# The recurrent gates of the first two tiles moved behind the products of the low-rank queries

## The chip, the cores and the metric

The program runs on one core of a Trainium2 chip, as one launch. The metric is the device time in microseconds (us), the median of several runs. The core has five engines, each with its own stream of instructions: PE (TensorE, matrix products), DVE (VectorE), ACT (ScalarE, with loadable function tables), POOL (GpSimd) and SP (SyncE, which here issues nearly all DMAs). They wait for each other by semaphores.

## The reference, cut to what matters

Two blocks follow each other on 1024 tokens of width 1024, in fp32: a block of two layers (a mixer of a gated recurrence and low-rank attention, then a state-space layer), and a second block (two feed-forward parts and a mixer). The change lies in the first mixer only:

```
proj = x @ w_in
x_rnn, gate, c_q, c_kv, k_rope = split(proj)          # 512, 1024, 256, 128, 32 columns
x_rnn = causal_conv(x_rnn, conv_w, conv_b)            # 4 taps
r = sigmoid(x_rnn @ w_a + b_a);  i = sigmoid(x_rnn @ w_x + b_x)
log_a = -8 * r * softplus(-lam);  a = exp(log_a)
u = sqrt(-expm1(2 * log_a)) * (i * x_rnn)
h[t] = a[t] * h[t-1] + u[t]                           # y_rnn
q  = rmsnorm(c_q, q_norm) @ w_uq
kv = rmsnorm(c_kv, kv_norm) @ w_ukv
... attention over 8 heads, then concat(y_rnn, y_mla) * silu(gate) @ w_out
```

## The kernel before, in words

Activations of the mixer stand feature by feature: a tile has 128 features (partitions) by 1024 tokens. A product that must be near fp32 is made from three: every factor is split into a high and a low part (`split`, lines 140 and 141: ACT copies the high part, DVE subtracts it), and high by high, high by low and low by high are added up in PSUM. A projection of one tile (`proj_fm`, line 185) is thus 8 blocks of features by 3 products by 2 halves of the tokens, 48 matmuls of 512 columns, into one PSUM tile `pa` of 1024 columns. The pool of these, `psA`, has two buffers; a second pool, `psB`, has four buffers `pb` of 512 columns.

`layer_a` starts with the projections of the first two recurrent tiles together (line 446, one product into each of the two `pa` buffers). `rnn(m)` then finishes recurrent tile m, for m from 0 to 3:

- the convolution `conv4`: ACT writes the first tap from `pa` (line 354), DVE adds three taps, each read from `pa` again (line 356);
- the gates: four plain fp32 matmuls of 512 columns from the convolved tile into `pb` (line 462), each followed by a Sigmoid on ACT (line 463);
- the rest: `i * xc` on DVE (line 464), Exp, Tanh and Sqrt on ACT (465 to 467), and on DVE lines 468 to 472, the last one the scan over the tokens. Sigmoid, Exp with Tanh, and Sqrt are in different function tables, so that ACT loads a table between them.

`low(...)` projects the low-rank queries (two tiles) or keys and values (one tile): product, Copy and Square on ACT (486, 487), a sum of squares by 8 matmuls with one column each (489), a root on DVE over 8 columns (493 to 283), that root spread over partitions by matmuls (501), a scaling on DVE (504) and a split. The program calls rnn(0), rnn(1), low for the queries, rnn(2), low for the keys, rnn(3), the rotary part and four gate tiles. Weights come by SP's DMAs into two staging buffers and are split into four buffers `whi` and four `wlo`.

The order on each engine is not the order of the calls: a scheduler places instructions by a model of their times, and may let a later product run ahead of something that waits. `turn(K, trace)` (line 168) takes this freedom away on PE: what `trace` issues is put behind the last PE instruction written before it.

Of the kernel before, what the change touches and what calls it, by code (L numbers as in the profile page):

```python
# [18 lines left out]
P = 128  # L19
# [3 lines left out]
NK = D // P  # L23
# [75 lines left out]
def anchor(K, engine=None):  # L99

    for i in reversed(K.nc.cur_bb.bb.instructions):
        if i.engine == (engine or K.pe):
            return i
    return None
# [33 lines left out]
def split(K, hi, lo, src, eng=None):  # L138

    K.nc.scalar.activation(hi, src, AF.Copy)  # L140
    (eng or K.nc.vector).tensor_tensor(lo, src, hi.bitcast(F32), ALU.subtract)  # L141


def scale_rows(K, st, gain, k0, n):

    for k in range(n):
        K.nc.scalar.activation(st[:, k, :], st[:, k, :], AF.Copy, scale=col(K, gain, k0 + k))  # L147


def wload(K, src, a, b, gain=None, k0=0):  # L150

    n = a * b
    st = K.pwst.tile([P, 1024], F32, tag="wst", name=K.nm("wst"))
    hi = K.pwh.tile([P, 1024], F32R, tag="whi", name=K.nm("whi"))
    lo = K.pwl.tile([P, 1024], F32R, tag="wlo", name=K.nm("wlo"))
    K.nc.sync.dma_start(st[:, :n].rearrange("p (a b) -> p a b", a=a), src)
    if gain is not None:
        scale_rows(K, st[:, :n].rearrange("p (a b) -> p a b", a=a), gain, k0, a)
    split(K, hi[:, :n], lo[:, :n], st[:, :n])
    v = lambda t: t[:, :n].rearrange("p (a b) -> p a b", a=a)  # L160
    return v(hi), v(lo)


def kp(ap):
    return ap.rearrange("(k p) c -> p k c", p=P)


def turn(K, trace):

    with K.tc.issue_after(anchor(K)):  # L170
        trace()


def proj_list(K, ps, terms, mid=None):


    n = len(terms)
    with ExitStack() as st:
        for k, (wh, wl, xh, xl) in enumerate(terms):
            if mid is not None and k == n // 2:  # L180
                turn(K, mid)
                st.enter_context(K.tc.issue_after(anchor(K)))
            for m, (w, x) in enumerate(((wh, xh), (wh, xl), (wl, xh))):
                for h in (0, 512):
                    K.nc.tensor.matmul(ps[:, h:h + 512], w, x[:, h:h + 512],  # L185
                                       start=k == 0 and m == 0, stop=k == n - 1 and m == 2)


def proj_fm(K, ps, w, xt, nk=NK, mid=None):
    proj_list(K, ps, [(w[0][:, k, :], w[1][:, k, :], xt("h", k), xt("l", k)) for k in range(nk)], mid)  # L190
# [34 lines left out]
def col(K, name, j=0, n=1, p0=0, p1=P):  # L225
    c0, _ = _PK[name]
    return K.pk[p0:p1, c0 + j:c0 + j + n]
# [36 lines left out]
def rsqrt_col(K, out, v, n, scale, eps, mul=1.0, tag="rs"):  # L264

    V = K.nc.vector
    t = K.small(3 * n, f"{tag}{n}", bufs=2 if n == 1 else 1)
    h, y, c = (t[:, j * n:(j + 1) * n] for j in range(3))  # L270
    k = 1.5 ** 0.2
    f = -0.5 / (mul * mul)
    V.tensor_scalar(h, v, scale * f, eps * f, ALU.mult, ALU.add)

    magic = 1597463007.0 - 2.0 ** 30 - 2.0 ** 22 + 2.0 ** 23 * math.log2(k) / 3
    V.tensor_scalar(y.bitcast(I32), h.bitcast(I32), -0.5, magic, ALU.mult, ALU.add)

    if n == 1:

        step = lambda o, i, a, b: V.tensor_scalar(o, i, a, b, ALU.add, ALU.mult)  # L280
        square = lambda: V.tensor_scalar(c, y, y, h, ALU.mult, ALU.mult)
    else:
        step = lambda o, i, a, b: V.scalar_tensor_tensor(o, i, a, b, ALU.add, ALU.mult)

        def square():
            V.tensor_tensor(c, y, y, ALU.mult)
            V.tensor_tensor(c, c, h, ALU.mult)

    square()
    step(y, c, 1.5 * k ** (2.0 / 3), y)  # L290
    square()
    step(h, c, k ** 2 * 5.0 / 3, c)
    step(out, h, k ** 4 * 1.25, y)
# [51 lines left out]
def conv4(K, out, src, wname, j, nm, bname, copy=False):  # L345


    nc = K.nc
    w = lambda k: col(K, wname, k * nm + j)
    raw = src  # L350
    if copy:
        raw = K.pwl.tile([P, 1024], F32, tag="wlo", name=K.nm("raw"))
        nc.scalar.activation(raw, src, AF.Copy)
    nc.scalar.activation(out, src, AF.Identity, bias=col(K, bname, j), scale=w(3))
    for s in (1, 2, 3):
        nc.vector.scalar_tensor_tensor(out[:, s:], raw[:, :T - s], w(3 - s), out[:, s:], ALU.mult, ALU.add)
# [58 lines left out]
def layer_a(K, I, XT, get):  # L415
    nc = K.nc

    w_in = kp(I["w_in"])
# [31 lines left out]
    def rnn(m):  # L450
        if m < 2:
            a = first[m]
        else:
            a = K.A()
            proj_fm(K, a, wload(K, w_in[:, :, m * P:(m + 1) * P], NK, P), get)
        pa, pb = K.P2(), K.P2()
        xc, t, i, s = pa[:, 0, :], pa[:, 1, :], pb[:, 0, :], pb[:, 1, :]
        conv4(K, xc, a, "a_conv_w", m, 4, "a_conv_b")
        for dst, w, b in ((t, m, "ga_b"), (i, 4 + m, "gx_b")):
            for h in (slice(0, 512), slice(512, 1024)):  # L460
                g = K.B()
                nc.tensor.matmul(g, wgv[:, w, :], xc[:, h], start=True, stop=True)
                nc.scalar.activation(dst[:, h], g, AF.Sigmoid, bias=col(K, b, m))
        nc.vector.tensor_tensor(i, i, xc, ALU.mult)
        nc.scalar.activation(xc, t, AF.Exp, scale=lam[:, 8 + m:9 + m])
        nc.scalar.activation(t, t, AF.Tanh, scale=lam[:, 4 + m:5 + m])
        nc.scalar.activation(s, t, AF.Sqrt)
        nc.vector.scalar_tensor_tensor(s, xc, 1.0, s, ALU.add, ALU.mult)
        nc.vector.tensor_tensor(i, i, s, ALU.mult)
        nc.vector.scalar_tensor_tensor(xc, xc, 1.0, t, ALU.add, ALU.mult)  # L470
        nc.vector.tensor_scalar(xc, xc, -1.0, 1.0, ALU.mult, ALU.add)
        nc.vector.tensor_tensor_scan(s, xc, i, 0.0, ALU.mult, ALU.add)
        return s


    rst = {}

    def low(c0, nt, name, scale):
        raws = []
        rq = K.Q2()  # L480
        ssq = K.B()
        for m in range(nt):
            a = K.A()
            proj_fm(K, a, wload(K, w_in[:, :, c0 + m * P:c0 + (m + 1) * P], NK, P), get)
            raw, sq = rq[:, m, :], K.S()
            nc.scalar.activation(raw, a, AF.Copy)
            nc.scalar.activation(sq, a, AF.Square)
            for i in range(NT):
                nc.tensor.matmul(ssq[:, m * 8 + i:m * 8 + i + 1], sq[:, i * P:(i + 1) * P], K.ones, start=True, stop=True)
            raws.append(raw)  # L490
        r = K.small(8, "rst" + name, bufs=1)
        v = K.small(8, "rsv" + name, bufs=1)
        nc.vector.tensor_copy(v, ssq[:, 0:8])
        for m in range(1, nt):
            nc.vector.tensor_tensor(v, v, ssq[:, m * 8:m * 8 + 8], ALU.add)
        rsqrt_col(K, r, v, 8, scale, 1e-6)
        outs = [K.Q2(F32R) for _ in range(nt)]
        for h in range(2):
            b = K.B()
            for q in range(4):  # L500
                nc.tensor.matmul(b[:, q * P:(q + 1) * P], r[:, 4 * h + q:4 * h + q + 1].to_broadcast([P, P]), K.ident, start=True, stop=True)
            for m in range(nt):
                rw = raws[m][:, h * 512:h * 512 + 512]
                nc.vector.scalar_tensor_tensor(rw, rw, col(K, name, m), b, ALU.mult, ALU.mult)
                split(K, outs[m][:, 0, h * 512:h * 512 + 512], outs[m][:, 1, h * 512:h * 512 + 512], rw)
        return outs

    hs = [rnn(0)]
    hs.append(rnn(1))
    cq = low(1536, 2, "qn", 1.0 / 256)  # L510
    hs.append(rnn(2))
    ckv = low(1792, 1, "kvn", 1.0 / 128)
    hs.append(rnn(3))
    cs, n1, n2 = K.R2(), K.L(), K.L()
    sin_tables(K, I["pos"], cs[:, 0, :], cs[:, 1, :], n1, n2)
    kr = K.A()
# [1446 lines left out]
def tile_two_blocks(ctx, tc, I, out):  # L1963
# [4 lines left out]

    XT, get = new_xt(K)
    ydram, zd = layer_a(K, I, XT, get)  # L1970
    XT = _Late(K)
    layer_a_out(K, I, ydram, zd, x1, XT)
# [46 lines left out]
```

## Time and profile before

| what | us |
|---|---|
| median of 3 runs (3287.15 to 3292.08) | 3291.51 |
| the profiled execution: time | 3285.83 |
| its span | 3284.10 |
| PE busy in it (94% of the span) | 3077.9 |
| DVE busy (67%) | 2211.5 |
| ACT busy (49%) | 1625.5 |
| POOL busy (24%) | 778.3 |

The times of rows are counted from the start of the span. PE is the engine that is nearly always busy, so in a stage where nothing else ends last a change counts by what it adds to or takes from PE's idle time and PE's clock. The first mixer's part up to the heads of attention takes the first 258 us.

### The profile page before, as it was taken

Reading aid. Unit: us, or ns where it says so; the run is one execution under the profiler, and the core shown is the slowest. Engines: PE = TensorE matmul, PEld = TensorE weight load, DVE = VectorE, ACT = ScalarE, POOL = GpSimd, SP = SyncE. Lnnn points to the kernel's source line nnn. Section 1 sums busy time; section 2 is a strip of 40 time slices with the busy share of each in tenths; the row PEclk is TensorE's granted clock in tenths of the full one; section 3 lists DMA queues with packets and bytes.
Section 4 is the critical chain, followed back from the end, with each engine's and each line's share of the span. In section 5 each row is a group of like instructions: output and inputs, shape, how many; then the busy total and the mean of one; then the engine's idle time right before and its main releaser. Section 6 shows DMA issues by size and latency. Waiting matters only on the chain. (4 is left out here: it accounts for less than half of the span.)

```text
span 3284.1 us, 42186 instructions
## 1 busy us (share of the span) xinstructions
PE 3077.9 (94%) x15560; PEld 2568.7 (78%) x15560; DVE 2211.5 (67%) x3637; ACT 1625.5 (49%) x2945; POOL 778.3 (24%) x487
## 2 busy tenths in 40 slices
PE   8999889999999989789999899899999799999998
PEld 6887777888897878578778777788787688888776
DVE  6537777356757556887775789736666955555997
ACT  5526543445555522655555443642565755554442
POOL 0000001113222221522233534100000432332543
PEclk9998999999999999899999999999999899999999
DMA  4157442334344565323332620354564322224223
GB/s 130 55 182 231 123 132 86 88 83 124 83 117 92 170 176 162 99 97 116 109 123 77 225 84 33 128 179 174 152 169 140 131 84 90 77 84 152 105 84 116
DMA packets 349567, 398.98 MB, mean 121 GB/s; under 512 B 21168, under 2 KB 279344, under 8 KB 349360
## 3 DMA queue, kind: packets, MB, share of 16 engines
q1 hardware_dynamic: 324016, 379.50, 37.1%
q10 hardware_dynamic: 25344, 16.78, 1.6%
q8 instruction: 123, 2.02, 0.3%
q14 instruction: 84, 0.69, 0.1%
HBM read 279.29 MB, written 116.92 MB: 121 GB/s over the span
## 5 line engine op out<-in xcount | busy, mean ns | idle before, releaser
L141 DVE TENSOR_TENSOR wlo<-wst,whi 128x1024 fp32r<-128x1024 f32 (+1 forms) x190 | 232.1, 1224 | 355.6 <-ACT whi L140 337.5
L185 PE MATMUL pa<-x,whi 128*128 128x512 f32 x1568 | 429.2, 395 | 1.8 <-DVE l L141 0.8
L140 ACT ACTIVATE whi<-wst 128x1024 fp32r<-128x1024 f32 (+1 forms) x190 | 180.1, 948 | 345.5 <-PE pa L185 86.0
L147 ACT ACTIVATE wst<-wst,pk 128x128 f32<-128x128 f32 (+1 forms) x816 | 251.7, 391 | 187.9 <-DMA wst<-in_ffn_w_in_dram 120.7
L185 PEld LDWEIGHTS pa<-x,whi 128*128 128x128 f32 x1568 | 292.0, 189 | 64.1 <-DVE x L141 1.8
L185 PE MATMUL pa<-x,wlo 128*128 128x512 f32 x784 | 244.2, 392 | 4.0 <-DVE wlo L141 4.0
L1325 PE MATMUL pa<-x,whi 128*128 128x512 f32 (+1 forms) x736 | 221.7, 384 | 4.2 <-ACT p L679 2.0
L1325 PE MATMUL pb<-x,whi 128*128 128x512 f32 (+1 forms) x736 | 224.0, 381 | 0.3 <-DVE r L141 0.3
L1404 PE MATMUL pa<-wlo,whi 128*128 128x512 f32 x768 | 188.5, 403 | 14.6 <-DVE wlo L141 12.7
L1404 PE MATMUL pb<-wlo,whi 128*128 128x512 f32 x744 | 182.2, 403 | 14.2 <-DVE wlo L141 14.2
L1288 POOL TENSOR_TENSOR s<-wst 128x512 f32<-128x512 f32 x44 | 57.9, 1317 | 561.2 <-ACT wst L147 525.4
L1404 PEld LDWEIGHTS pa<-wlo,whi 128*128 128x128 f32 x768 | 148.4, 194 | 52.3 <-DVE wlo L141 18.4
L1404 PEld LDWEIGHTS pb<-wlo,whi 128*128 128x128 f32 x744 | 143.9, 195 | 48.5 <-DVE wlo L141 18.2
L185 PEld LDWEIGHTS pa<-x,wlo 128*128 128x128 f32 x784 | 147.0, 188 | 38.8 <-DVE wlo L141 7.4
L937 POOL TENSOR_TENSOR s<-s,p 128x1024 f32<-128x1024 f32 x32 | 65.6, 2051 | 440.7 <-DMA s<-d 324.5
L1325 PEld LDWEIGHTS pa<-x,whi 128*128 128x128 f32 x736 | 136.8, 190 | 32.0 <-issue 2.6
L1325 PEld LDWEIGHTS pb<-x,whi 128*128 128x128 f32 x736 | 135.9, 188 | 26.9 <-DVE r L141 0.5
L140 ACT ACTIVATE whi<-s 128x1024 fp32r<-128x1024 f32 x88 | 93.0, 1057 | 117.5 <-POOL s L1289 67.1
L891 PE MATMUL pa<-whi,x 128*128 128x256 f32 x512 | 147.9, 289 | 0.0
L892 PE MATMUL pa<-wlo,x 128*128 128x256 f32 x512 | 145.1, 283 | 1.9 <-DVE wlo L141 1.9
L893 PE MATMUL pa<-whi,x 128*128 128x256 f32 x512 | 144.8, 283 | 0.0
L681 POOL TENSOR_TENSOR p<-p,q 128x1024 f32<-128x1024 f32 x8 | 21.1, 2641 | 515.0 <-DVE p L680 476.4
(591 smaller groups left out, 8056.9 us busy)
## 6 DMA issues: line engine op xcount, KB each, us to landing
wst<-in_ffn_w_in_dram SPq DMA_DIRECT2D x88, 512.0 KB, 3.8
d<-p SPq DMA_DIRECT2D x82, 512.0 KB, 3.5
d<-l SPq DMA_DIRECT2D x67, 512.0 KB, 3.9
x<-d SPq DMA_DIRECT2D x128, 256.0 KB, 5.4
p<-d SPq DMA_DIRECT2D x46, 512.0 KB, 4.7
wst<-in_s_w_in_dram SPq DMA_DIRECT2D x40, 512.0 KB, 4.0
s<-d SPq DMA_DIRECT2D x32, 512.0 KB, 9.6
l<-d SPq DMA_DIRECT2D x24, 512.0 KB, 5.6
```

The costliest lines, as they stand in the source:

```text
L140: K.nc.scalar.activation(hi, src, AF.Copy)
L141: (eng or K.nc.vector).tensor_tensor(lo, src, hi.bitcast(F32), ALU.subtract)
L147: K.nc.scalar.activation(st[:, k, :], st[:, k, :], AF.Copy, scale=col(K, gain, k0 + k))
L185: K.nc.tensor.matmul(ps[:, h:h + 512], w, x[:, h:h + 512], start=k == 0 and m == 0, stop=k == n - 1 and m == 2)
L681: nc.gpsimd.tensor_tensor(z, z, b, ALU.add)
L891: nc.tensor.matmul(o, xh, wh, start=k == 0, stop=False)
L892: nc.tensor.matmul(o, xh, wl, start=False, stop=False)
L893: nc.tensor.matmul(o, xl, wh, start=False, stop=k == NK - 1)
L937: nc.gpsimd.tensor_tensor(mv, mv, per_head(csT, P), ALU.subtract)
L1288: G(s1, a21, a22, ALU.add)
L1325: nc.tensor.matmul(p, l[:, k, :], r[:, k, :], start=k + m == 0, stop=k == 3 and m == 2)
L1404: nc.tensor.matmul(bank[j], th[:, a + o:a + o + P], tw[:, b:b + 512], start=c + m == 0, stop=c == n - 1 and m == 2)
```

## The change

`rnn` becomes a generator with a stop behind the convolution and a second one at its result. The first two tiles are convolved first. `low` for the queries gets a list of two traces, one for each of its two products: behind the sum of squares of a product comes the rest of one recurrent tile (gates, Exp, Tanh, Sqrt, scan). Each product of `low`, and each of these rests, is put in place with `turn`. rnn(2) and rnn(3) run through at once, as before; `low` for the keys has no list, but its product stands in a `turn` as well.

```diff
@@ -456,6 +456,7 @@
         conv4(K, xc, a, "a_conv_w", m, 4, "a_conv_b")
+        yield
         for dst, w, b in ((t, m, "ga_b"), (i, 4 + m, "gx_b")):
...
         nc.vector.tensor_tensor_scan(s, xc, i, 0.0, ALU.mult, ALU.add)
-        return s
+        yield s
...
-    def low(c0, nt, name, scale):
+    def low(c0, nt, name, scale, behind=()):
...
-            proj_fm(K, a, wload(K, w_in[:, :, c0 + m * P:c0 + (m + 1) * P], NK, P), get)
+            w = wload(K, w_in[:, :, c0 + m * P:c0 + (m + 1) * P], NK, P)
+            turn(K, lambda: proj_fm(K, a, w, get))
...
             raws.append(raw)
+            if behind:
+                turn(K, behind[m])
...
-    hs = [rnn(0)]
-    hs.append(rnn(1))
-    cq = low(1536, 2, "qn", 1.0 / 256)
-    hs.append(rnn(2))
+
+    hs = []
+    pair = [rnn(0), rnn(1)]
+    for r in pair:
+        next(r)
+    cq = low(1536, 2, "qn", 1.0 / 256, [lambda r=r: hs.append(next(r)) for r in pair])
+    hs.append(list(rnn(2))[-1])
     ckv = low(1792, 1, "kvn", 1.0 / 128)
-    hs.append(rnn(3))
+    hs.append(list(rnn(3))[-1])
```

On PE, behind the two products of the first tiles (`pa_199`, `pa_200`), there stood before the gates of tile 0 (from `p_297`), the first product of the queries (`pa_353`), and the gates of tile 1 (from `p_324`) in its last pair:

```order
L446 MATMUL pa_200<-x_115,wlo_128 128x512
L462 MATMUL pb_303<-p_297,r_197 128x512
...
L462 MATMUL pb_312<-p_297,r_197 128x512
L185 MATMUL pa_353<-x_114,whi_355 128x512 x2
...
L185 MATMUL pa_353<-x_115,wlo_356 128x512
L462 MATMUL pb_330<-p_324,r_197 128x512
```

There now stand the first product of the queries (`pa_311`), its sum of squares, the gates of tile 0, and the second product (`pa_398`):

```order
L446 MATMUL pa_200<-x_115,wlo_128 128x512
L185 MATMUL pa_311<-x_114,whi_313 128x512 x2
...
L185 MATMUL pa_311<-x_115,wlo_314 128x512 x2
L491 MATMUL pb_310<-ones,s_366 128x1 x8
L463 MATMUL pb_377<-p_297,r_197 128x512
...
L463 MATMUL pb_386<-p_297,r_197 128x512
L185 MATMUL pa_398<-x_114,whi_400 128x512 x2
```

The gates of tile 0 moved behind a product and its sum of squares, and this sum, which stood in the middle of the next product, now stands directly behind its own.

Further on, on PE, the product of recurrent tile 2 is `pa_523`, its convolved tile `p_578`, and the product of the keys `pa_607`. Before, that product stood on both sides of the queries' root (line 501) and of the gates of tile 2:

```order
L185 MATMUL pa_607<-x_114,whi_609 128x512 x2
...
L501 MATMUL pb_512<-ident,rstqn_485 128x128 x4
L185 MATMUL pa_607<-x_116,whi_609 128x512 x2
...
L462 MATMUL pb_584<-p_578,r_197 128x512
...
L185 MATMUL pa_607<-x_117,whi_609 128x512 x2
```

Now the end of `pa_523` (with the last gate of tile 1, `pb_473`), the root, the gates and the whole product follow one another:

```order
L463 MATMUL pb_473<-p_303,r_197 128x512
L185 MATMUL pa_523<-x_117,whi_525 128x512
L185 MATMUL pa_523<-x_115,wlo_526 128x512 x2
L505 MATMUL pb_501<-ident,rstqn_485 128x128 x4
L505 MATMUL pb_512<-ident,rstqn_485 128x128 x4
L463 MATMUL pb_584<-p_578,r_197 128x512
...
L463 MATMUL pb_593<-p_578,r_197 128x512
L185 MATMUL pa_607<-x_114,whi_609 128x512 x2
```

No matmul of the keys' product stands ahead of the gates of tile 2 any more.

On DVE, at the same place, the three taps of tile 2 (line 356, from `pa_523`) stood before among the scalings of the queries (line 504), and the second half of tile 1 had been done long before:

```order
L356 SCALAR_TENSOR_TENSOR p_578<-pa_523,pk,p_578 128x1023
L356 SCALAR_TENSOR_TENSOR p_578<-pa_523,pk,p_578 128x1022
L504 SCALAR_TENSOR_TENSOR q_351<-q_351,pk,pb_501 128x512 x2
L356 SCALAR_TENSOR_TENSOR p_578<-pa_523,pk,p_578 128x1021
L504 SCALAR_TENSOR_TENSOR q_351<-q_351,pk,pb_512 128x512 x2
```

Now the taps stand apart, and ahead of the last of them is line 469 for tile 1 (`p_303`, `p_304`), which reads the Sqrt:

```order
L508 SCALAR_TENSOR_TENSOR q_309<-q_309,pk,pb_512 128x512 x2
L356 SCALAR_TENSOR_TENSOR p_578<-pa_523,pk,p_578 128x1023
L141 TENSOR_TENSOR q_499<-q_309,q_499 128x512
...
L141 TENSOR_TENSOR q_500<-q_309,q_500 128x512
L356 SCALAR_TENSOR_TENSOR p_578<-pa_523,pk,p_578 128x1022
L469 SCALAR_TENSOR_TENSOR p_304<-p_303,p_304 128x1024
L356 SCALAR_TENSOR_TENSOR p_578<-pa_523,pk,p_578 128x1021
```

The last tap of tile 2 moved behind an instruction of tile 1 that waits for ACT. Lines from 459 on are numbered 1 to 7 higher in the changed kernel.

## Rows read from the trace of the kernel before

**Rows 1.** Waits of PE, longest in total: line, releaser, us in total, times, longest.

```profile
PE pb L462 <- issue: 6.3, 1, 6.3
```

**Rows 2.** Timeline of PE: start, us, instructions merged, in brackets the idle time before.

```profile
32.69 0.39 PE L446 MATMUL pa<-x,wlo 128*128 128x512 f32 x1
39.38 6.10 PE L462 MATMUL pb<-p,r 128*128 128x512 f32 x8 [6.31 <-issue]
...
50.80 1.07 PE L185 MATMUL pa<-x,whi 128*128 128x512 f32 x4
...
52.16 1.07 PE L185 MATMUL pa<-x,whi 128*128 128x512 f32 x4
...
71.96 0.62 PE L185 MATMUL pa<-x,wlo 128*128 128x512 f32 x2
...
88.31 1.95 PE L501 MATMUL pb<-ident,rstqn 128*128 128x128 f32 x16
90.02 0.71 PE L185 MATMUL pa<-x,whi 128*128 128x512 f32 x2
```

**Rows 3.** Timeline of DVE, the convolutions, the recurrence and the scalings.

```profile
36.69 2.59 DVE L356 SCALAR_TENSOR_TENSOR p<-pa,pk,p 128x1022 f32<-128x1022 f32 x2
...
53.68 1.23 DVE L468 SCALAR_TENSOR_TENSOR p<-p,p 128x1024 f32<-128x1024 f32 x1 [2.27 <-ACT p L467]
54.94 1.23 DVE L469 TENSOR_TENSOR p<-p 128x1024 f32<-128x1024 f32 x1
...
89.63 1.40 DVE L504 SCALAR_TENSOR_TENSOR q<-q,pk,pb 128x512 f32<-128x512 f32 x2
...
93.45 2.49 DVE L141 TENSOR_TENSOR q<-q,q 128x512 fp32r<-128x512 f32 x4
```

**Rows 4.** Timeline of ACT: gates, tables, and what follows a product.

```profile
44.66 0.69 ACT L463 ACTIVATE p<-pb,pk 128x512 f32<-128x512 f32 x1 [0.80 <-PE pb L462]
45.24 1.21 ACT L354 ACTIVATE p<-pa,pk 128x1024 f32<-128x1024 f32 x1
46.33 0.69 ACT L463 ACTIVATE p<-pb,pk 128x512 f32<-128x512 f32 x1
...
48.93 1.16 ACT L465 ACTIVATE p<-p,lam 128x1024 f32<-128x1024 f32 x1 [0.61 <-DVE p L464]
...
51.29 1.28 ACT L467 ACT_TABLE_LOAD   x1
52.59 1.06 ACT L467 ACTIVATE p<-p 128x1024 f32<-128x1024 f32 x1
...
72.16 1.06 ACT L140 ACTIVATE whi<-wst 128x1024 fp32r<-128x1024 f32 x1 [3.52 <-PE pa L185]
73.13 1.01 ACT L486 ACTIVATE q<-pa 128x1024 f32<-128x1024 f32 x1
74.03 1.02 ACT L487 ACTIVATE s<-pa 128x1024 f32<-128x1024 f32 x1
...
85.85 1.19 ACT L354 ACTIVATE p<-pa,pk 128x1024 f32<-128x1024 f32 x1
...
90.41 1.35 ACT L140 ACTIVATE q<-q 128x512 fp32r<-128x512 f32 x2 [3.36 <-DVE q L504]
```

**Rows 5.** Stretches: length, busy us of PE, PEld, DVE, ACT, POOL, granted clock, DMA.

```profile
39.30:45.00 5.70, 5.62 (x9) 2.49 (x9) 0.00 (x0) 2.77 (x4) 0.00 (x0) 0.56 0.17 48
...
1230.80:1238.00 7.20, 7.19 (x26) 5.80 (x27) 6.08 (x11) 1.74 (x4) 1.04 (x1) 0.76 0.40 130
...
1653.70:1661.00 7.30, 7.28 (x34) 6.04 (x35) 7.30 (x12) 5.77 (x14) 0.00 (x0) 1.00 0.34 99
```

**Rows 6.** Timeline of PE, two waits of 2.5 to 2.7 us elsewhere.

```profile
1230.81 0.49 PE L941 MATMUL pb<-q 128*128 128x128 f32 x2 [2.73 <-ACT r L1000]
...
1653.72 0.70 PE L1325 MATMUL pa<-r,whi 128*128 128x512 f32 x2 [2.48 <-DVE p L1334]
```

**Rows 7.** The stretch that holds the heads of attention, columns as in rows 5.

```profile
260.00:500.00 240.00, 218.74 (x1275) 189.90 (x1275) 175.40 (x376) 126.67 (x280) 8.40 (x4) 0.95 0.51 152
```

## The prediction

> **What bounds the kernel now.** I read the busy shares first: PE is busy for 94% of the span, so what counts is PE's idle time and its clock. The list of PE's waits came second. In the part that the change touches it has one entry of size [rows 1], and the timeline of PE shows where it is [rows 2]: the last matmul of the first two products starts at 32.69 and lasts 0.39, and PE then stands still for 6.31 us until the gates of tile 0 start at 39.38. The releaser is named "issue", but the timeline of DVE tells more [rows 3]: the second and third tap of tile 0 run from 36.69 for 2.59 us, to 39.28, and the gates read the convolved tile. After this hole the clock is low: between 39.3 and 45.0 the granted clock is 0.56 on the mean [rows 5], that is a time at 1.2 and the rest at 2.4 GHz, which costs 5.70 x (1 - 0.56) = 2.5 us. The hole and its clock are 8.8 us in all. From 45 to beyond 200 us the timeline marks no further wait of PE, since the scheduler has put the other gates, sums and the root into the middle of products. Every microsecond that PE stands still there later is therefore added to the time.
>
> The pitch of a matmul at the high clock is (52.16 - 50.80) / 6 = 0.227 us [rows 2], a product of 48 is 10.9 us.
>
> **The change part by part.** The matmuls are the same in number and kind. What changes is what PE meets in its order, so I follow the order of the changed program and take each duration from the rows.
>
> *First hole.* PE now goes from the first products to pa_311. That product needs no convolved tile, but it needs a PSUM tile. The pool psA has two, both hold the first products, and the taps read them from there. The buffer of pa_199 comes free when DVE has done the last tap of tile 0, which is the very instruction that released the gates. And DVE now has one tap of tile 1 ahead of it: 2.59 / 2 = 1.3 us [rows 3]. So the hole does not close, it grows from 6.3 to 7.6 us: **+1.3**. If ACT's first tap of tile 1 were late this would be more, but that needs only pa_200, which is complete at 33.1, and stands third in ACT's order. The low clock behind the hole falls on pa_311 and no longer on the gates, at the same price: 0, with -1 to +1 as bounds.
>
> *Second hole.* The sum of squares of pa_311 needs its Copy and its Square, and nothing may fill the time, because the gates of tile 0 stand behind the sum and pa_398 behind the gates. Before, this time lay under the next product. Its size is read from the same three instructions [rows 4]: high part of a weight at 72.16, Copy at 73.13, Square at 74.03 for 1.02, end at 75.05. The product concerned ended, in pitch, at 71.96 + 2 x 0.227 = 72.41 [rows 2]. The distance is 2.64, with 0.06 for the release **+2.7**. The weight split counts here, because it waits for a buffer that pa_311 gives free and stands ahead of the Copy. For the second product of the queries pa_523 may run ahead, 31 of its matmuls by the order, so 7.0 us cover it: nothing there.
>
> *The clock after the second hole.* The trace has waits of this length with either outcome [rows 5, 6]: behind 2.48 us at 1653.72 the next 7.3 us have clock 1.00, behind 2.73 us at 1230.81 the next 7.2 us have 0.76, which is 1.7 us. Ends 0 and 2.5 (the price after the long hole); I take the middle of the two near rows, **+0.9**. The Trainium skill ("TensorE: Matmul & The Clock Gate", section "HAM oscillation") says that short idle times between groups of matmuls lower the clock again and again. The 0.76 agrees and the 1.00 does not; by that rule alone the term would be 2.5 and the sum 1.6 larger.
>
> *Third hole.* Here the keys' product pa_607, which before surrounded the root and the gates of tile 2, stands wholly behind these gates, since its turn hangs on the last PE instruction written before it. Between pa_523 and the gates PE has only the root, 90.02 - 88.31 = 1.7 us [rows 2]. The gates need all taps of tile 2, and the last tap stands on DVE behind line 469 of tile 1, which reads the Sqrt of tile 1. That Sqrt is late, because the last gate of tile 1 (pb_473) stands three matmuls before the end of pa_523. I count from that end, in pitch. The Sigmoid of pb_473 is over at about -0.4 (the gate ends 3 x 0.227 and a change of operands of some 0.4 earlier, and it takes 0.69). ACT then has in a row [rows 4]: the high part of a weight to 0.8; first tap of tile 2, 1.1 more, to 1.9; table load 1.3, to 3.2; Exp 1.16, to 4.35; two copies of the queries 1.3, to 5.65; Tanh, an ACTIVATE of the Exp's size, to 6.75; two copies to 8.05; table load to 9.35; Sqrt 1.06, to 10.4. DVE's own work until there is shorter [rows 3]: a product of 1.2, four scalings 2 x 1.4, a weight split 1.2, a tap 1.3, four splits 2.5 and a tap 1.3 end near 9.9. Then come line 469, in pitch 54.94 - 53.68 = 1.26, to 11.7, and the last tap 1.3, so the gates start at 13.0. Less the root, PE is idle for **+11.3**. Before, the gates of tile 2 waited for nothing. Bounds: if neither ACT nor DVE kept to its order, the taps alone would end at 1.9 + 3 x 1.3 = 5.8, an idle time of 4.1; if pb_473 comes a Sigmoid later, 12. That an engine keeps its order is seen on ACT: at 44.66 it had sat idle 0.80 for a gate, while line 354 of tile 1, whose product was complete at 33.1, stood behind and ran at 45.24 [rows 4]. So I take 11.3.
>
> *The clock after it.* A wait longer than the 6.31 us, so the price of that one [rows 5]: **+2.5**, bounds 1.5 and 3.5.
>
> The two table loads in this chain are counted with 1.28 and 0.02 to the next ACTIVATE (51.29 to 52.59, rows 4). The Trainium skill ("ScalarE: Activation LUTs", section "What ACT_TABLE_LOAD costs") gives about 2.66 us for every switch, a drain included; an estimate by it would make the third hole 2.7 longer. The row disagrees and decides.
>
> *Small edits.* The gates of tile 1 are cut in two by a product, those of tile 3 no longer are: +0.4 and -0.4. Weights: the split of the root product's weight comes late on ACT, but the buffers are four deep, nothing waits. SP's loads keep their order there. The scan of tile 2 and the second half of its gates come some 10 us later than the first, but their reader is a gate tile two products and more away: 0.
>
> *Downstream.* From pa_703 on the order is nearly the old one until the heads, where the scheduler has written another order for about four of the eight heads. From 260 to 500 us PE is idle 240 - 218.7 = 21.3 us, and the clock of 0.95 costs 12 more [rows 7]. A different order can give back a part of that or add to it. I see no reason for a sign: 0, bounds -12 (a third of it back) and +10.
>
> The sum is 1.3 + 2.7 + 0.9 + 11.3 + 2.5 = 18.7 us. Against the profiled execution that is 3285.83 + 18.7 = 3304.5. The three timed runs have their median 5.7 above that execution; the mean of the four known times is 3289.1, and on it the forecast is 3308.
>
> **The rivals.** *The order of the heads gives back what the stage lost.* Place: the heads rewritten by the scheduler; price: at most the 33 us of rows 7, decisive from about 12, where the result is no longer distinguishable from no change. For it: 33 us of idle time and clock are there to win. Against it: its waits are many small ones and the heads' work is the same. With 17 back: 3291, not slower.
>
> *The first hole closes.* If pa_311 could start at 33.1, the 6.3 us and their 2.5 us of clock go, and the 1.3 with them: 18.7 - 10.1 = 8.6, 3298. This is what a product ahead of gates should give. Against it: the two tiles of psA, both being read until 39.3 or later.
>
> *The heads lose as well:* +10, 3318. For it: a new order that the scheduler made by its own times; against it as in the first rival.
>
> **How the numbers follow.** A measurement of this kernel cannot tell less than about 0.2% (6.6 us) from no change. Chances: my forecast 0.72 (its own range 3299 to 3316, from the bounds of the clock terms and of the base), heads give back 0.10, first hole closes 0.05, heads lose 0.13. The first rival is half of it inside 0.2% and one third faster, the second lies at the edge. Faster 0.04, same 0.09, slower 0.87. The range reaches into both neighbours: 3294 to 3321.
>
> **What would show it.** In the changed profile PE should wait about 7.6 us before pa's first matmul of line 185, with DVE's line 356 as releaser; about 2.5 us before line 491, released by the Square; about 11 us before line 463 for tile 2, released by line 356; and the clock should be low behind the first and the third. On DVE line 469 should wait for the Sqrt between two taps. The product behind the keys' one (pa_703) should start some 19 us later than before. I am wrong if the first wait is gone, if the third is under 6 us, or if the mixer's heads start about 18 us later and the time is yet the same.

## The result, and the profile of the changed kernel

The changed kernel takes 3315.99 us (median of 4, 3311.84 to 3319.24) against 3291.51 of the kernel before on the same chip: a ratio of 1.0084 with a 95% interval of 1.0070 to 1.0099, or 23 to 33 us more on 3291.51. The forecast was 3308 in a range of 3294 to 3321. The profiled execution took 3311.84, its span is 3310.1, and PE is idle for 3310.1 - 3080.1 = 230.0 us of it; before it was 206.2.

Beside all later runs the kernel before takes about 3281 us, 0.3% less than the 3291.51 above; no run tells why. So every kernel below is compared with the executions of the kernel before that were timed beside it, and each ratio is to those.

The timeline of PE (start, us, instructions merged, in brackets the idle time before) has three waits of size in the part that the change touches, in the place of the one of [rows 1, 2]:

```profile
39.84 2.04 PE L185 MATMUL pa<-x,whi 128*128 128x512 f32 x4 [7.41 <-DVE p L356]
...
54.84 2.24 PE L491 MATMUL pb<-ones,s 128*128 128x1 f32 x16 [2.52 <-ACT s L489]
56.95 5.07 PE L463 MATMUL pb<-p,r 128*128 128x512 f32 x8
...
88.93 1.95 PE L505 MATMUL pb<-ident,rstqn 128*128 128x128 f32 x16
...
101.70 6.57 PE L463 MATMUL pb<-p,r 128*128 128x512 f32 x8 [10.82 <-DVE p L356]
```

The first wait now stands before the first product of the queries and is 1.1 us longer than the 6.31 that the gates of tile 0 had. DVE answers to [rows 3]: it runs five taps in one piece, the last two of tile 0 and all three of tile 1. The third of the five ends at 39.8 (36.05 + 2 x 1.22 + 1.28), where PE starts, so one tap of tile 1 stands ahead of the last one of tile 0. What the third wait waits for is the last line below, behind line 469 of tile 1.

```profile
36.05 6.16 DVE L356 SCALAR_TENSOR_TENSOR p<-pa,pk,p 128x1022 f32<-128x1022 f32 x5
...
97.66 1.28 DVE L356 SCALAR_TENSOR_TENSOR p<-pa,pk,p 128x1022 f32<-128x1022 f32 x1
99.14 1.23 DVE L469 SCALAR_TENSOR_TENSOR p<-p,p 128x1024 f32<-128x1024 f32 x1 [0.20 <-ACT p L468]
100.28 1.28 DVE L356 SCALAR_TENSOR_TENSOR p<-pa,pk,p 128x1021 f32<-128x1021 f32 x1
```

ACT's timeline (compare [rows 4]) has both causes that were added: at 51.91 to 54.79 the split, the Copy and the Square that PE waits for ahead of the sum of squares, and from 88.43 the chain that ends in the Sqrt.

```profile
51.91 1.06 ACT L140 ACTIVATE whi<-wst 128x1024 fp32r<-128x1024 f32 x1 [12.39 <-PE pa L185]
52.87 1.00 ACT L488 ACTIVATE q<-pa 128x1024 f32<-128x1024 f32 x1
53.78 1.01 ACT L489 ACTIVATE s<-pa 128x1024 f32<-128x1024 f32 x1
...
88.43 0.69 ACT L464 ACTIVATE p<-pb,pk 128x512 f32<-128x512 f32 x1 [3.37 <-PE pb L463]
...
91.17 1.28 ACT L466 ACT_TABLE_LOAD   x1
92.47 1.15 ACT L466 ACTIVATE p<-p,lam 128x1024 f32<-128x1024 f32 x1
...
96.75 1.28 ACT L468 ACT_TABLE_LOAD   x1
98.05 1.06 ACT L468 ACTIVATE p<-p 128x1024 f32<-128x1024 f32 x1
```

Stretches of the changed kernel (length, busy us of PE, PEld, DVE, ACT, POOL, granted clock, DMA; compare [rows 5]): behind each of the three waits, then from the end of the first two products to the start of the heads, then the heads.

```profile
39.80:47.00 7.20, 7.16 (x26) 5.84 (x27) 2.37 (x2) 0.00 (x0) 0.00 (x0) 0.80 0.01 2
55.00:60.00 5.00, 5.00 (x20) 3.35 (x21) 0.00 (x0) 1.78 (x2) 0.00 (x0) 0.66 0.37 105
101.70:109.00 7.30, 7.30 (x12) 3.44 (x13) 5.11 (x4) 2.75 (x4) 0.00 (x0) 0.60 0.00 0
...
32.40:275.50 243.10, 216.52 (x929) 172.10 (x929) 111.54 (x122) 102.44 (x110) 0.00 (x0) 0.94 0.32 105
...
275.50:501.40 225.90, 203.88 (x1201) 177.91 (x1202) 161.16 (x339) 122.20 (x270) 5.79 (x2) 0.95 0.50 151
```

The same two stretches of the kernel before:

```profile
33.10:258.50 225.40, 213.85 (x929) 171.07 (x929) 111.22 (x122) 102.23 (x110) 0.00 (x0) 0.97 0.34 113
...
258.50:484.30 225.80, 204.00 (x1200) 177.52 (x1201) 161.74 (x344) 121.42 (x270) 5.80 (x2) 0.95 0.52 152
```

The stretch up to the heads is 243.1 - 225.4 = 17.7 us longer. PE's idle time in it grows from 225.40 - 213.85 = 11.55 to 243.10 - 216.52 = 26.58, that is by 15.0, of which the three waits make 7.41 + 2.52 + 10.82 - 6.31 = 14.4; the other 2.7 is busy time of the same 929 matmuls, so the clock. The heads are equally long in these two traces. Of the 26.0 us by which the spans differ, 8.9 lie behind the heads (3310.1 - 501.4 against 3284.1 - 484.3), and the first products end 0.7 us earlier in the changed kernel.

### The profile page after: what moved, and what is told of

It reads as the page before. It is cut to its first block, busy times and chain, and to the rows that moved or that the text cites. A ratio compares the mean times of both kernels' runs of the same rounds, so it can differ in the third digit from the quotient of the medians.

```text
span 3310.1 us, 42197 instructions
## 1 busy us (share of the span) xinstructions
PE 3080.1 (93%) x15560; PEld 2573.4 (78%) x15560; DVE 2211.4 (67%) x3637; ACT 1627.8 (49%) x2945; POOL 775.9 (23%) x487
## 5 line engine op out<-in xcount | busy, mean ns | idle before, releaser
L1332 PE MATMUL pa<-x,whi 128*128 128x512 f32 (+1 forms) x736 | 221.5, 383 | 2.1 <-ACT l L1629 1.6
```

The source lines that it names most:

```text
L1332: nc.tensor.matmul(p, l[:, k, :], r[:, k, :], start=k + m == 0, stop=k == 3 and m == 2)
```

## The experiments

Each kernel is the one before or the changed one with the edit shown. I read two lengths in every trace: the first mixer, from the last matmul of the first two products (line 446) to the first matmul of the heads (line 381), and the heads, from there to the first matmul of line 212. They are given at the end in one table, against a repeat of the kernel before.

**The keys' product without its turn** (in the changed kernel):

```diff
-            turn(K, lambda: proj_fm(K, a, w, get))
+            if behind:
+                turn(K, lambda: proj_fm(K, a, w, get))
+            else:
+                proj_fm(K, a, w, get)
```

> The changed kernel, but the product of the keys is not pinned behind the gates of recurrent tile 2. By my theory the third wait of PE (10.8 us in the changed kernel, before the gates of tile 2) and the low clock behind it are due to that pin: the product of 10.9 us now stands ahead of those gates and covers the wait, so that it falls under 1 us, PE starts the following projection about 13 us earlier than in the changed kernel, and the time is 13 us below it: about 3303, some 12 above the kernel before. Waits one and two stay (7.4 and 2.5 us). Rival: DVE and ACT are simply late there (the tail of tile 1 stands in front of the taps), and the wait only moves on to the next product, whose PSUM buffer the taps hold: then at least 8 us of idle time come back within the next 15 us and the time stays within 4 us of the changed kernel's. On the late stages: they lost some 7 us in the changed kernel beside the mixer; if that is due to their rewritten order, it stays here, since this kernel has the same late order.

Measured: 3297.97, ratio 1.0045 (1.0030 to 1.0059). The third wait is gone, the other two have stayed:

```profile
40.76 2.04 PE L185 MATMUL pa<-x,whi 128*128 128x512 f32 x4 [7.42 <-DVE p L356]
...
56.40 1.95 PE L494 MATMUL pb<-ones,s 128*128 128x1 f32 x16 [2.52 <-ACT s L492]
```

The third wait hangs on the one turn of the keys' product. With that product free, all its 48 matmuls stand between the root and the gates of tile 2, from 92.21 to the start of the gates at 103.29. DVE's order is still that of the changed kernel, with the last tap behind line 469. This tap ends at 103.1, which is 12.6 us behind the start of the root, as in the changed kernel; but PE now has work until then.

**The turn of the keys' product alone** (in the kernel before, where the second half of tile 1 is done long before):

```diff
+            w = wload(K, w_in[:, :, c0 + m * P:c0 + (m + 1) * P], NK, P)
+            if nt == 1:
+                turn(K, lambda: proj_fm(K, a, w, get))
+            else:
+                proj_fm(K, a, w, get)
```

> The kernel before, with one part of the change alone: the product of the keys pinned behind the gates of tile 2. By my theory the first wait stays at 6.3 us, there is no second one, and the third appears: taps behind the weight split, four scalings and four splits of the queries, so about 9.4 us idle and 2.5 us of low clock, time 12 above the kernel before, about 3303. If the third wait of the changed kernel was due to the tail of tile 1 on ACT and DVE, which is long done here, the wait is the taps alone, 4 us, and the time at most 5 to 6 above the kernel before.

Measured: 3300.97, ratio 1.0061 (1.0048 to 1.0074). The wait is there without any part of the pair of tiles being moved:

```profile
96.05 6.69 PE L462 MATMUL pb<-p,r 128*128 128x512 f32 x8 [9.00 <-DVE p L356]
```

DVE's order shows what the 9.00 consists of when tile 1 isn't in it, the scalings and splits of the queries:

```profile
87.07 2.72 DVE L508 SCALAR_TENSOR_TENSOR q<-q,pk,pb 128x512 f32<-128x512 f32 x4
89.71 1.28 DVE L356 SCALAR_TENSOR_TENSOR p<-pa,pk,p 128x1023 f32<-128x1023 f32 x1
90.90 2.49 DVE L141 TENSOR_TENSOR q<-q,q 128x512 fp32r<-128x512 f32 x4
93.31 2.59 DVE L356 SCALAR_TENSOR_TENSOR p<-pa,pk,p 128x1022 f32<-128x1022 f32 x2
```

So the turn makes 9.0 of the 10.8 us, and the late half of tile 1 ahead of the last tap adds 1.8. The time is 19.8 us above the kernel before, where 12 were expected: the mixer accounts for 12.5 of them, and the heads are longer too (see the table).

**No turns at all** (in the changed kernel; the generator and the two lists stay):

```diff
-            turn(K, lambda: proj_fm(K, a, w, get))
+            proj_fm(K, a, w, get)
...
-                turn(K, behind[m])
+                behind[m]()
```

> The changed kernel without any pin: the order of the calls is that of the change, but products may run ahead of sums and gates. By my theory the first wait stays (7.4 us, a product waits for the PSUM buffer of tile 0), the second and third go: the mixer is about 1 to 2 us slower than in the kernel before and the time within 3 us of it, unless the late stages add their own. If the first wait were caused by the pins, it would be gone and the mixer 7 to 9 us faster than before.

Measured: 3296.92, ratio 1.0046 (1.0034 to 1.0058). A miss: the mixer should have come within a few us of the kernel before, and lost more. The first wait stays, the sum of squares is covered again, and a wait for the gates of tile 2 shows up where I had expected none:

```profile
40.90 2.04 PE L185 MATMUL pa<-x,whi 128*128 128x512 f32 x4 [7.42 <-DVE p L356]
...
104.16 6.58 PE L463 MATMUL pb<-p,r 128*128 128x512 f32 x8 [5.06 <-DVE p L356]
```

The scheduler has put the whole keys' product ahead of these gates, and on DVE the late half of tile 1 (its scan alone is 2.28) between the taps of tile 2:

```profile
93.74 1.28 DVE L356 SCALAR_TENSOR_TENSOR p<-pa,pk,p 128x1023 f32<-128x1023 f32 x1
...
96.84 1.27 DVE L356 SCALAR_TENSOR_TENSOR p<-pa,pk,p 128x1022 f32<-128x1022 f32 x1
...
99.35 2.28 DVE L473 TENSOR_TENSOR_SCAN p<-p,p 128x1024 f32<-128x1024 f32 x1
...
102.74 1.27 DVE L356 SCALAR_TENSOR_TENSOR p<-pa,pk,p 128x1021 f32<-128x1021 f32 x1
```

The third wait thus has two makers: the turn, which is enough by itself, and a second half of tile 1 that comes late. The late half makes a wait of its own where, as here, its scan stands ahead of the last tap. With the keys free and the other turns kept, only line 469 stood there, and the keys' product covered it.

**The two products of the queries in their turn, the rests of the tiles free** (in the changed kernel; the keys free too):

```diff
-            turn(K, lambda: proj_fm(K, a, w, get))
+            if behind:
+                turn(K, lambda: proj_fm(K, a, w, get))
+            else:
+                proj_fm(K, a, w, get)
...
-                turn(K, behind[m])
+                behind[m]()
```

> The changed kernel with pins on the two products of the queries only; the gates and the product of the keys are free. By my theory waits one and two stay (7.4 and 2.5 us, with clock about 5 us above the kernel before), wait three goes. The heads of attention have the order of the kernel before again. Time about 3296, plus what the late stages add; if their loss came with the rewritten order of the stage near 1370 us, of which this kernel has a milder form, that is under 4 us; if it comes with any shift of the start, it is the same 7 us as in the changed kernel.

Measured: 3296.48, ratio 1.0043 (1.0031 to 1.0055). The first two waits are there with their old sizes (7.42 and 2.52), and one of 3.77 is left before the gates of tile 2, where none was expected:

```profile
106.99 6.62 PE L463 MATMUL pb<-p,r 128*128 128x512 f32 x8 [3.77 <-DVE p L356]
```

The second wait therefore does not hang on the turn of the tiles' rests; with the turns of the two products alone the sum of squares has no matmul beside it either. The third wait is that of the kernel without turns: on DVE the scan of tile 1 stands again ahead of the last tap. So the mixer is 11.3 us longer, not about 5.

**The changed kernel with the first two products copied out of PSUM** (this adds one ACTIVATE for each of the two tiles; the taps then read the copy):

```diff
+        if m < 2:
+            raw = K.S()
+            nc.scalar.activation(raw, a, AF.Copy)
+            a = raw
         conv4(K, xc, a, "a_conv_w", m, 4, "a_conv_b")
```

> The changed kernel, with the first two products copied from PSUM by ACT (1.05 us each) into a tile in SBUF that the convolution then reads. By my theory the first wait of PE is for the PSUM buffer of tile 0 and not for the convolution as such: it falls from 7.4 to about 1.2 us, and the low clock behind it goes with it; waits two and three stay at 2.5 and about 11 us. Time 7 to 9 us below the changed kernel's distance from the kernel before, so about +18 instead of +25 to +27. Rival: the product waits for something else that the convolution sets free (a weight or a split on DVE); then the wait stays above 6 us.

Measured: 3300.66, ratio 1.0060 (1.0042 to 1.0079). The first wait is 0.47 and ends with the copy of the first product; the others are what they were:

```profile
33.49 1.20 PE L185 MATMUL pa<-x,whi 128*128 128x512 f32 x4 [0.47 <-ACT s L460]
...
47.18 3.49 PE L495 MATMUL pb<-ones,s 128*128 128x1 f32 x16 [2.52 <-ACT s L493]
...
95.66 5.08 PE L467 MATMUL pb<-p,r 128*128 128x512 f32 x8 [10.82 <-DVE p L356]
```

The mixer is 7 us shorter for it. What the first product of the queries waited for is the PSUM tile that the taps hold, and nothing else.

**The kernel before with the same two copies:**

```diff
+        if m < 2:
+            raw = K.S()
+            nc.scalar.activation(raw, a, AF.Copy)
+            a = raw
```

> The kernel before, with nothing but that copy of the first two products out of PSUM. The scheduler then lets the first product of the queries run ahead of the gates of tile 0 by itself, without any pin. By my theory PE's first wait falls from 6.3 to about 1.2 us with no low clock behind it, no other wait appears, and the mixer is 6 to 8 us faster than in the kernel before; the whole is then 3 to 8 us faster if the late stages stay, and about even if they lose their 4 to 8 us by any shift of the start.

Measured: 3282.43, ratio 1.0005 (0.9996 to 1.0014). The 6.31 us are gone (0.47 is left), a wait of 2.86 at 81.00 for the queries' root has come, and the mixer is shorter, yet the time is the same: the heads took 233.6 us in this trace. "About even" was the outcome expected if any shift of the start lost time later; the delayed kernel below speaks against that reason.

**The kernel before, once more**, to see how far two traces of one kernel differ:

> The kernel before once more, for a trace on the same chip as the runs beside it. Both theories of the late stages need it: its stages must be those of the first trace within 2 us each if the chips are alike, and may differ by some us in single stages by the place of the low-clock stretches alone.

Measured: 3282.93 in the profiled execution, with the same single wait of 6.31 at 39.51. Its heads are 220.3 us long against 225.8 in the first trace, and that is the largest difference between the two, more than the 2 us that were expected of a stage.

**The kernel before, its start delayed** (17 copies of an idle tile ahead of the first weight; the rival that any shift by some 20 us loses time later):

```diff
-    first = [wload(K, w_in[:, :, 0:P], NK, P)]
+    idle = K.S()
+    nc.vector.memset(idle, 0.0)
+    for _ in range(17):
+        nc.scalar.activation(idle, idle, AF.Copy)
+    idle_end = K.nc.cur_bb.bb.instructions[-1]
+    with K.tc.issue_after(idle_end):
+        first = [wload(K, w_in[:, :, 0:P], NK, P)]
```

> The kernel before with 17 copies on ACT (some 1.06 us each, on a tile that nothing else reads) spread among its first weight and activation splits; the mixer behind the first two products and the heads keep the order of the kernel before, but the scheduler writes the same changed order into the late stages as in the kernel with only the queries' products pinned. Theory A (late stages lose with the rewritten order or with any shift): the time behind the first products grows by 4 to 8 us over that of the kernel before, apart from the delay itself. Theory B (the loss of the late stages in the changed kernel comes from its own mixer and heads): from the last matmul of the first products to the end it stays within 2 us of the kernel before. The delay ahead of that matmul should be 10 to 18 us, as a part of the copies finds room.

Measured: 3302.93, ratio 1.0068 (1.0048 to 1.0088). The delay itself was larger than I had worked out: the first matmul starts at 30.31 against 8.13 in the repeat of the kernel before, that is 22.2 us:

```profile
30.31 2.17 PE L452 MATMUL pa<-x,whi 128*128 128x512 f32 x4 [30.31 <-ACT whi L140]
```

From the last matmul of the first two products to the last one of the program this trace is 3.5 us shorter than that of the repeat, and the median is 22.05 us above that of the kernel before (3302.93 - 3280.88), which is the delay alone. Being late costs nothing more.

**The changed kernel, once more:**

> The changed kernel once more, on the chip of this call, for its distance from the kernel before on the same chip and for its stages: from the first products to the heads 17 to 19 us longer than before, over the heads some 3 to 8 us longer than the 220 to 226 us of the kernels that keep the old order of the heads, and 24 to 28 us in all.

Measured: 3307.74, ratio 1.0078 (1.0064 to 1.0093). The waits are 7.41, 2.52 and 10.82 again, and the mixer is 0.1 us from the first trace's.

**The kernel before with only tile 0 copied:**

```diff
+        if m < 1:
+            raw = K.S()
+            nc.scalar.activation(raw, a, AF.Copy)
+            a = raw
```

> The kernel before, with the first product alone copied out of PSUM by ACT ahead of its convolution. The scheduler then puts the first product of the queries ahead of the gates of tile 0; the heads and all later stages keep the order of the kernel before but for three rows. By my theory the first wait falls from 6.3 to about 1.3 us, the mixer is 6 to 8 us faster and, since the heads keep their order, the whole is 5 to 9 us faster than before (0.15 to 0.27%). If the late stages lose with any change of the start, and not with the heads' new order, it is within 3 us of the kernel before, as the kernel with both copies and the new heads was.

Measured: 3278.95, ratio 0.9991 (0.9982 to 0.9999). The mixer gained less than expected, since a later product of line 185 now waits 3.91 us for the Square of a product of the queries, which stands late in ACT's order. The whole gained 2.2 us, not 5 to 9. That is within the 3 us named for the case that the late stages lose with any change, but the heads have kept their length here (see the table):

```profile
34.22 1.20 PE L185 MATMUL pa<-x,whi 128*128 128x512 f32 x4 [0.47 <-ACT s L460]
...
52.75 2.08 PE L185 MATMUL pa<-x,whi 128*128 128x512 f32 x4 [3.91 <-ACT s L491]
```

**The kernel before with both tiles copied, into a buffer of the weights' pool.** On PE the heads then have the very order of the kernel before:

```diff
+        if m < 2:
+            raw = K.pwl.tile([P, 1024], F32, tag="wlo", name=K.nm("raw"))
+            nc.scalar.activation(raw, a, AF.Copy)
+            a = raw
```

> The kernel before, with the first two products copied out of PSUM, this time into buffers of the low weight parts; heads and late stages then keep the order of the kernel before to the row. By my theory the first wait falls to about 2 us (the low part of the next weight waits for one of these buffers), the mixer is 5 to 7 us faster and the whole too, against the kernel with the same copies and the new heads' order, which was 4 us faster in the mixer and lost it again. If the loss is not the heads' order, this one is even with the kernel before as well.

Measured: 3276.15, ratio 0.9984 (0.9974 to 0.9994). This is the version that beats both kernels, by 5.0 us against the one before, near the edge of what can be measured. PE goes from the first products to the next one without a pause and meets the gates of tile 0 in its last pair:

```profile
33.27 0.39 PE L446 MATMUL pa<-x,wlo 128*128 128x512 f32 x1
33.50 1.11 PE L185 MATMUL pa<-x,whi 128*128 128x512 f32 x4
...
43.06 0.84 PE L185 MATMUL pa<-x,whi 128*128 128x512 f32 x3
43.74 3.59 PE L466 MATMUL pb<-p,r 128*128 128x512 f32 x8
```

**All of them in one table.** Mixer and heads are lengths in us against the repeat of the kernel before, whose heads take 220.3; they are good to 0.1. "New" is the order that the heads' matmuls have on PE in the changed kernel, row for row; "old" that of the kernel before.

| kernel | heads' order on PE | mixer | heads | ratio of the times |
|---|---|---|---|---|
| before, first trace | old | +0.6 | +5.5 | |
| before, delayed | old, a few rows differ | -0.1 | +0.9 | 1.0068 (22.2 of delay) |
| only the query products in turn | old, a few rows differ | +11.3 | +2.2 | 1.0043 |
| before, tile 0 copied | old, a few rows differ | -2.3 | -0.2 | 0.9991 |
| before, both copied, weights' pool | old | -5.5 | -1.0 | 0.9984 |
| changed, first trace | new | +18.3 | +5.6 | 1.0084 |
| changed, again | new | +18.2 | +5.1 | 1.0078 |
| changed, keys free | new | +4.4 | +7.1 | 1.0045 |
| before, keys in turn | new | +12.5 | +6.1 | 1.0061 |
| changed, both copied | new | +11.2 | +6.4 | 1.0060 |
| before, both copied | new | -3.6 | +13.3 | 1.0005 |
| changed, no turns | another | +8.2 | +9.4 | 1.0046 |

The new order of the heads costs about 6 us: six traces of it lie between 225.4 and 233.6, mean 227.6; the six of the old and nearly old order between 219.3 and 225.8, mean 221.5. It comes with kernels whose mixer is early and late alike, and the delayed one keeps the old length, so it goes with the order and not with the shift. (ACT's and DVE's order of the heads changes together with PE's.) The times agree for the two kernels that differ least, the kernel before with both tiles copied: in the new order it is at 1.0005 (0.9996 to 1.0014), in the old one at 0.9984 (0.9974 to 0.9994). That is about 7 us apart, and the mixer makes 1.9 of it. Stretches with the columns as above, the heads of the changed kernel's repeat:

```profile
275.90:501.30 225.40, 204.03 (x1200) 177.93 (x1201) 160.68 (x338) 122.32 (x270) 5.80 (x2) 0.95 0.52 151
```

and in the last kernel, with the old order:

```profile
253.00:472.30 219.30, 198.30 (x1201) 171.85 (x1202) 160.43 (x338) 120.86 (x270) 5.80 (x2) 0.98 0.52 156
```

The difference between these two is nearly all in the busy time of the same matmuls, so in the clock (0.95 against 0.98), but the last kernel is the one with the least low clock. Over the six traces of each group PE's idle time in the heads is 21.4 to 25.2 us in the new order, mean 23.2, and 18.6 to 21.8 in the old, mean 20.0. Its busy time is 201.5 to 209.3, mean 204.3, against 198.3 to 204.0, mean 201.5. So about half of the 6 us is waiting and half is clock, and the clock scatters more than the two groups differ. The list of PE's waits in that stretch says where PE stops more often. The changed kernel's repeat:

```profile
PE pb L400 <- ACT p L140: 7.9, 11, 2.7
PE pb L394 <- DVE q L404: 4.2, 3, 1.6
...
PE pa L381 <- DVE ast L385: 2.5, 6, 1.3
```

and the repeat of the kernel before:

```profile
PE pb L400 <- ACT p L140: 8.5, 12, 2.3
...
PE pb L394 <- DVE q L404: 1.3, 1, 1.3
...
PE pa L381 <- DVE ast L385: 0.5, 2, 0.3
```

Line 394 waits for line 404 three times instead of once, and line 381 for line 385 five times as long; together 4.9 us more. The other traces agree: the first of these waits is 4.2 to 5.3 us in all six of the new order and 1.2 to 2.2 in the six of the old, the second 2.2 to 3.2 against 0.5 to 1.5. The wait of line 400 for line 140 is shorter in return, 7.3 to 8.2 us against 8.5 to 9.9. No run undid these rows of the order alone, so that they are what costs the time, and that they lower the clock, is argued and not shown.

## Why the prediction was right, point by point

**First hole.** Predicted to grow from 6.3 to 7.6, by one tap; it is 7.4 in the five traces that have it. The cause is shown: the copies take the taps' hold on the PSUM tile away, and with it the wait. As a way to run a product ahead of the gates the change could not work with two such tiles. The clock behind it was taken at the same price as before; it is 7.2 x (1 - 0.80) = 1.4 us where it was 2.5, so this term should have been -1. (The last section shows why the price differs.)

**Second hole.** Predicted 2.7, found 2.52, and released by the Square as said. The clock behind it was taken as 0.9, the middle of two rows; it is 5.0 x (1 - 0.66) = 1.7. The Trainium skill ("TensorE: Matmul & The Clock Gate", section "A second HAM failure mode: psum-queue depth-cycling", the one behind the section that the prediction names) says that frequent short idle times of PE between groups of matmuls let the clock fall and rise again and again. The waits here are single ones: behind the 2.52 us and the 2.73 of [rows 6] the clock fell, behind the 2.48 there it did not, so the rule did not decide the term.

**Third hole.** Predicted 11.3, found 10.82, with gates that start 12.8 us after the last product's end (88.9 to 101.7) against 13.0 in the working. ACT's chain came in the order and nearly at the durations that were added up, and DVE held the last tap behind line 469, which waited 0.20 us for the Sqrt. Its two table loads took 1.28 each, and the next ACTIVATE started 0.02 behind them. The larger price of the Trainium skill ("ScalarE: Activation LUTs", section "What ACT_TABLE_LOAD costs"), by which the wait is estimated at about 14, does not agree with this trace. The runs correct the attribution: the turn of the keys' product alone makes 9.0 of it, and tile 1's late half 1.8. The clock behind it was taken as 2.5, and is 7.3 x (1 - 0.60) = 2.9.

**The sum of the mixer** was 18.7. It is 17.7 and 17.6 in the two traces of the changed kernel, against the trace that the prediction had; the terms as measured, 1.1 - 1.1 + 2.5 + 1.7 + 10.8 + 2.9, add up to 17.9.

**Downstream.** This is the term that was mis-sized: taken as 0, with -12 and +10 as bounds. Against the trace that the prediction had, the heads came out equal (225.8 and 225.9), but that trace was 5.5 us long in its heads, as the repeat shows; the new order costs about 6. The rival "the heads lose as well", given 0.13 and +10, is thus half of the truth. With 18.2 for the mixer and 5.1 for the heads the repeat of the changed kernel is at 23.3, and its span is 3304.1 - 3281.2 = 22.9 above that of the repeat of the kernel before. That accounts for the whole difference of these two executions. The measured 3315.99 is 8 us above the forecast, at the very end of the forecast's own range (3299 to 3316); the stated range, 3294 to 3321, holds it with room to spare because it reaches into the rival "the heads lose". So the mixer was forecast by its mechanism, and the rest of the time was caught by the width of the range.

**What stays open.** From the end of the heads to the last matmul, the first trace of the changed kernel takes 8.6 us more than the first trace of the kernel before, where its repeat takes 2.7 more and the repeat of the kernel before 3.1 more; other kernels lie between -4 and +9 there. It does not follow the order, and no run told what it follows. For single kernels the sum of mixer and heads is off the timed difference by up to 8 us (both tiles copied: +9.7 in the trace, 0.05% or 1.6 us in the times), so the 6 us hold for the group, not for one trace.

**The rivals.** The heads gave nothing back. The first hole did not close in the changed kernel; where both copies closed it, the mixer gained 7.1 in the changed kernel and 3.6 to 5.5 in the one before (by the table), less than the 8.8 us of hole and clock. In the changed kernel the clock behind the second wait is low for longer (0.51 over the 7.0 us from 47.2); in the kernel before with both tiles copied, other stops came up, as the 2.86 us before the root.

## What to carry to other kernels

A product that is to run ahead of a wait needs its own output tile: look at who still reads the tiles of its pool before reordering, since a copy that frees the tile early can do what the new order can't. An instruction that is pinned in place can take away the cover of what follows: list what the scheduler had put into its middle, and price that work as a bare wait on the engines' own order. And a change near the front lets a scheduler rewrite a part far behind it; a second trace of the kernel before, timed against the first, tells how much of such a part's length is the order's and how much is scatter.

## What the runs showed of the hardware

The clock behind a wait does not follow its length here. Behind 7.41 us of standing still it was 0.80 for 7.2 us, behind 6.31 it was 0.56 for 5.7 [rows 5], and behind 2.52 us, with a sum of one-column matmuls next, 0.66 for 5.0. Behind 10.82 it was 0.60 for 7.3. In the copied version of the changed kernel the same 2.52 us have matmuls of line 495 behind them that take 3.49 us, against 2.24.

What counts is how much of the low stretch is left when PE starts again. In the changed kernel the clock is at 0.50, that is at 1.2 GHz, while PE still stands in the first wait, and stays there for the first 2.9 us of work; from 42.7 to 47.0 it is 1.00:

```profile
35.90:39.80 3.90, 0.00 (x0) 0.00 (x0) 3.90 (x5) 3.59 (x4) 0.00 (x0) 0.50 0.58 169
39.80:42.70 2.90, 2.86 (x7) 2.31 (x8) 2.37 (x2) 0.00 (x0) 0.00 (x0) 0.50 0.03 6
```

In the kernel before, the 0.50 covers the last 1.8 us of the shorter wait (37.5 to 39.3) and then 5.0 us of work (39.3 to 44.3). So the longer wait had the smaller price, because more of its low stretch passed while PE had nothing to do. The prediction took the price of one wait for another and could not see this from a single mean clock.
